# Rewriting a fused hybrid layer (short convolution plus latent attention) on eight cores: a new deal of the tokens, a new order of the stages, and row sums moved off TensorE

## The chip, the cores and the metric

The kernel runs on all 8 cores of one Trainium2 chip. Cores 0 to 3 (one die) work on the first sequence of the batch, cores 4 to 7 (the other die) on the second, and no core talks to another. The metric is device time in microseconds (us) of the slowest core.

Executions come in two states. In the fast one, all cores have nearly the same granted TensorE clock and nearly the same span (0.975 to 0.978 and 3345.0 to 3367.5 us in the profiled run of before). In the slow one, the cores of one die or of both have a lower clock and the time is longer (one die at 0.806 to 0.813 in the slowest run of before, 3942.61 us). A ratio is the mean time of one kernel's fast runs over that of the other's fast runs of the same rounds on the same chip, so it is not quite the ratio of the medians that are quoted.

## The reference, cut to what matters

```python
D_MODEL, BATCH, SEQ, CHUNK = 4096, 2, 4096, 64
N_HEADS, Q_LORA, KV_LORA, ROPE_DIM = 16, 1024, 512, 64     # nope and value: 128 per head

xn = rmsnorm(x, g_in)
proj = xn @ w_in
gB, gC, h, z_conv, c_q, c_kv, k_rope, z_attn = split(proj)
y_conv = gB * causal_short_conv(gC * h, conv_w) * silu(z_conv)     # depthwise, width 3
q = rmsnorm(c_q, q_norm_g) @ w_uq          # 16 heads of 128 + 64
kv = rmsnorm(c_kv, kv_norm_g) @ w_ukv      # 16 heads of 128 + 128
# rope on q_pe and on the one shared k_rope; mask by chunks: key_chunk <= query_chunk
attn = softmax(q k^T / sqrt(192), masked) @ v
y = concat(y_conv, attn * silu(z_attn))
out = rmsnorm(x + y @ w_out, g_final)
```

A core owns 1024 query tokens of its sequence, but needs the latent keys (`c_kv` and `k_rope`) of all 4096. The mask is causal by chunks of 64 tokens.

## The kernel before

Each core owns two blocks of 512 tokens: block k and block 7-k. It computes the stages in this order: latent keys of all 4096 tokens, query and gate projections, attention, convolution, output projection. Between them stand barriers, and the convolution reads x again, since attention takes its room.

Latent keys, with the features on the partitions (the weights are the stationary operand, 512 tokens stream through):

```python
for m in range(5):                       # 4 tiles of c_kv, 1 of duplicated rope columns: 640
    for kc in range(32):
        mm(psb[bank], WCKV[:, kc, m*128:(m+1)*128], XG[xb][:, kc, :], ...)
# sum of squares: 32 more matmuls per slot with a matrix of ones
mm(psb[0], ones_bf, xsq[stb][:, j, :], ...)
...
mm(psb[4], dmat, tk, True, True, ...)    # fp32 product that adds the rope halves
```

Attention, per head and key tile. One program serves all cores, so blocks that a core's mask forbids are computed too and set to zero by a bias in the exponential (`gate`). The row sums of the softmax are a third matmul, with a matrix of ones:

```python
units = [(0, 0), (1, 1), (2, 2), (3, None)]            # block bi == 0: (slot, gate column)
# bi == 1: [(0..3, None), (4, 3), (5, 4), (6, 5), (7, None)]; 48 key tiles of 128 per head
mm(psb[bank][:, c0:512], KH[...], QN[...]); mm(psb[bank][:, c0:512], K2[...], TQ[...])
P.add("act", ... activation(out=PT[pb], in_=psb[bank], func=AF.Exp, bias=gate[:, gc:gc+1]))
mm(psb[po][:, c0:512], VH[...], PT[pb][:, c0:512], ...)
mm(psb[pl][:, c0:512], ones_bf, PT[pb][:, c0:512], ...)      # row sums
```

Output projection, in two passes of 512 tokens, each of which reads all of `w_out` (4 MB per column tile of 512, 8 column tiles):

```python
for grp in range(2):
    for ct in range(8):
        for kg in range(8):
            ... mm(psb[pbase + tt], ysrc, wo[:, kcc, :], kc == 0, kc == 31)
    # norm of 4 row tiles, then the stores
```

The softmax here doesn't subtract the row's maximum and nothing guards it: scores larger than these inputs give would overflow.

Of the kernel before, what the change touches and what calls it, by code (L numbers as in the profile page):

```python
# [6 lines left out]
F32 = mybir.dt.float32  # L7
BF16 = mybir.dt.bfloat16
# [5 lines left out]
D = 4096  # L14
S = 4096
BLK = 512
NMT = 93
EPS = 1e-6
ATTN_SCALE = 192 ** -0.5
ORDER = [0, 1, 2, 4, 5, 6, 3, 7]  # L20
NEG = -30000.0

class Tr:
    __slots__ = ("lastw", "readers", "sem", "cnt", "name")

    def __init__(self, name=""):
        self.lastw = None
        self.readers = []
        self.sem = None
        self.cnt = 0  # L30
        self.name = name

class Ins:
    __slots__ = ("eng", "fn", "deps", "signal", "ordinal", "dma_tr", "dma_val")

    def __init__(self, eng, fn, deps):
        self.eng = eng
        self.fn = fn
        self.deps = deps
        self.signal = False  # L40
        self.ordinal = 0
        self.dma_tr = None
        self.dma_val = 0

ENGS = ("pe", "act", "dve", "pool", "sp")

class Prog:
    def __init__(self):
        self.ins = {e: [] for e in ENGS}
        self.last = {e: None for e in ENGS}  # L50
        self.dma_trs = []
        self.sync_same_engine = True

    def _deps(self, eng, reads, writes):
        deps = []
        for t in reads:
            if t.lastw is not None:
                deps.append(t.lastw)
        for t in writes:
            if t.lastw is not None:  # L60
                deps.append(t.lastw)
            deps.extend(t.readers)
        out = []
        for d in deps:
            if d[0] == "c":
                i = d[1]
                if i.eng == "pe" and eng == "pe":
                    continue
                if i.eng == eng and not self.sync_same_engine:
                    continue  # L70
                i.signal = True
            out.append(d)
        return out

    def add(self, eng, fn, reads=(), writes=()):
        ins = Ins(eng, fn, self._deps(eng, reads, writes))
        ev = ("c", ins)
        for t in reads:
            t.readers.append(ev)
        for t in writes:  # L80
            t.lastw = ev
            t.readers = []
        self.ins[eng].append(ins)
        self.last[eng] = ins
        return ins

    def dma(self, eng, fn, reads=(), writes=(), sem_tr=None):
        ins = Ins(eng, fn, self._deps(eng, reads, writes))
        if sem_tr is None:
            sem_tr = writes[0]  # L90
        if sem_tr not in self.dma_trs:
            self.dma_trs.append(sem_tr)
        sem_tr.cnt += 16
        ins.dma_tr = sem_tr
        ins.dma_val = sem_tr.cnt
        ev = ("d", sem_tr, sem_tr.cnt)
        for t in reads:
            t.readers.append(ev)
        for t in writes:
            t.lastw = ev  # L100
            t.readers = []
        self.ins[eng].append(ins)
        return ins

    def barrier(self):
        evs = []
        for e in ("pe", "act", "dve", "pool"):
            if self.last[e] is not None:
                self.last[e].signal = True
                evs.append(("c", self.last[e]))  # L110
        for t in self.dma_trs:
            evs.append(("d", t, t.cnt))
        for e in ENGS:
            self.ins[e].append(Ins(e, None, list(evs)))

    def emit(self, nc, stack):
        esem = {e: stack.enter_context(nc.semaphore("sem_" + e)) for e in ("pe", "act", "dve", "pool")}
        for i, t in enumerate(self.dma_trs):
            t.sem = stack.enter_context(nc.semaphore("dsem%d" % i))
        for e in ("pe", "act", "dve", "pool"):  # L120
            n = 0
            for i in self.ins[e]:
                if i.signal:
                    n += 1
                    i.ordinal = n
        block = stack.enter_context(nc.Block())

        def run(ename, eng):
            waited = {}
            for i in self.ins[ename]:  # L130
                for d in i.deps:
                    if d[0] == "c":
                        sem, val, key = esem[d[1].eng], d[1].ordinal, d[1].eng
                    else:
                        sem, val, key = d[1].sem, d[2], id(d[1])
                    if waited.get(key, 0) >= val:
                        continue
                    waited[key] = val
                    eng.wait_ge(sem, val)
                if i.fn is None:  # L140
                    continue
                r = i.fn(eng)
                if i.dma_tr is not None:
                    r.then_inc(i.dma_tr.sem, 16)
                elif i.signal:
                    r.then_inc(esem[ename], 1)
# [21 lines left out]
R_XG = 0  # L168
R_Y = 65536
R_CKVN = 131072  # L170
R_K2 = 163840
R_CQG = 172032
R_MISC = 188416
ARENA = 188416 + 20480 + 2048

def build_program(dbg=False):
    nc = bass.Bass("TRN2", target_bir_lowering=False)
    P = Prog()

# [3 lines left out]
    xT = din("xT", [8, 128, 32, 512])  # L183
    xres = din("xres", [1024, D])
    xh = din("xh", [128, 32, 4])
    cs_tab = din("cs_tab", [8, 128, 512])
    gate_d = din("gate", [128, 6])
    w_in_t = din("w_in_t", [NMT, 128, 32, 128])
    w_uq_t = din("w_uq_t", [16, 128, 8, 256])
    w_ukv_t = din("w_ukv_t", [8, 128, 4, 512])  # L190
    w_out_t = din("w_out_t", [8, 8, 128, 4, 512])
    g_in_d = din("g_in_t", [128, 32])
    g_q_d = din("g_q_t", [128, 8])
    g_kv_d = din("g_kv_t", [128, 4])
    convw_d = din("convw_t", [128, 48])
    gfin_d = din("gfin_b", [128, D])
    dmat_d = din("dmat", [128, 128])
    out = nc.dram_tensor("out", [1024, D], F32, kind="ExternalOutput").ap()

    stack = contextlib.ExitStack()  # L200
    with stack:
        arena = stack.enter_context(nc.sbuf_tensor("arena", [128, ARENA // 4], F32))
        psb_t = [stack.enter_context(nc.psum_tensor("psb%d" % i, [128, 512], F32)) for i in range(8)]
        psb = [t[:, :] for t in psb_t]
        tps = [Tr("ps%d" % i) for i in range(8)]

        def v32(off, n):
            return arena[:, off // 4: off // 4 + n]

        def v16(off, n):  # L210
            return arena[:, off // 4: off // 4 + n // 2].bitcast(BF16)

        mo = [R_MISC]

        def misc32(n):
            a = v32(mo[0], n)
            mo[0] += 4 * n
            return a

        def misc16(n):  # L220
            a = v16(mo[0], n)
            mo[0] += 2 * n
            return a

        g_in_t = misc32(32)
        g_q_t = misc32(8)
        g_kv_t = misc32(4)
        convw = misc32(48)
        gate = misc32(6)
        ssq = misc32(32)  # L230
        tot = misc32(4)
        rfin = misc32(4)
        rbh = misc32(4)
        rbh2 = misc32(4)
        uh = misc32(4)
        dmat = misc32(128)
        ones_bf = misc16(128)
        rb = [misc32(512) for _ in range(2)]
        cs = [misc32(512) for _ in range(2)]
        rqb = [misc32(512) for _ in range(2)]  # L240
        csq = [misc32(512) for _ in range(2)]
        rkvb = misc32(512)
        assert mo[0] <= ARENA, mo[0]
        t_const = Tr("const")
        t_rb = [Tr(), Tr()]
        t_cs = [Tr(), Tr()]
        t_rqb = [Tr(), Tr()]
        t_csq = [Tr(), Tr()]
        t_rkvb = Tr()
        t_small = Tr("small")  # L250

        XG = [v16(R_XG + b * 32768, 16384).rearrange("p (k t) -> p k t", k=32) for b in range(2)]
        t_xg = [[Tr() for _ in range(8)] for _ in range(2)]
        Y = v16(R_Y, 32768).rearrange("p (f t) -> p f t", f=32)
        t_y = [[Tr() for _ in range(2)] for _ in range(32)]
        CKVN = v16(R_CKVN, 16384).rearrange("p (k t) -> p k t", k=4)
        t_ckvn = [Tr() for _ in range(8)]
        K2 = v16(R_K2, 4096)
        t_k2 = [Tr() for _ in range(8)]
        CQG = v16(R_CQG, 8192).rearrange("p (k t) -> p k t", k=8)  # L260
        t_cqg = [[Tr() for _ in range(2)] for _ in range(8)]

        for dst, src in ((g_in_t, g_in_d), (g_q_t, g_q_d), (g_kv_t, g_kv_d), (convw, convw_d),
                         (gate, gate_d), (dmat, dmat_d)):
            P.dma("sp", lambda e, dst=dst, src=src: e.dma_start(out=dst, in_=src), writes=[Tr()])
# [101 lines left out]
        for _ in load_slot(0):  # L367
            pass
# [495 lines left out]
```

## Time and profile before

The time before was 3382.11 us (median of 3 runs, 3380.28 to 3384.14). These are the first lines of the profile's page of the kernel before, and its chain of waits: the span, the busy time of each engine with its share and number of instructions, and the engines' shares of the chain that ended last.

```profile
span 3367.5 us, 49842 instructions; the slowest of 8 cores (3345.0 to 3367.5 us)
PE 3026.4 (90%) x15163; PEld 1421.8 (42%) x15456; DVE 861.4 (26%) x1359; ACT 852.0 (25%) x1356; POOL 151.0 (4%) x249
PE 84%; DMA 11%; DVE 2%; issue 2%; ACT 1%; SPq 0%; DVEq 0%; ACTq 0%; POOLq 0%
```

TensorE (PE) is the bound: busy for 90% of the span and 84% of the chain (PEld are its own weight loads; they overlap its matmuls, since 3026.4 and 1421.8 us together are more than the span). No other engine is busy for a third of it. What the average hides is where TensorE stands still, and that a cut by stages shows. This is the view of time windows of core 6, cut at the stage boundaries: start and end, length, busy us of each engine, granted TensorE clock, share of DMA time, GB/s. The windows are, in this order: start, latent keys, query and gate projection, attention, the hole after it, convolution, output projection, tail.

```profile
0.00:102.90 102.90, 16.19 (x32) 2.22 (x33) 20.18 (x41) 23.00 (x22) 8.74 (x9) 1.00 0.97 172
102.90:470.00 367.10, 345.60 (x1521) 153.24 (x1552) 186.68 (x309) 140.24 (x138) 0.00 (x0) 0.99 0.47 156
...
486.90:855.60 368.70, 337.77 (x1521) 151.37 (x1552) 48.45 (x67) 32.12 (x50) 14.75 (x21) 1.00 0.37 66
...
865.00:1847.50 982.50, 968.82 (x5032) 490.17 (x5120) 300.46 (x444) 540.77 (x897) 10.57 (x20) 1.00 0.10 21
1847.50:1907.90 60.40, 1.02 (x33) 1.10 (x35) 22.34 (x41) 1.86 (x3) 2.11 (x3) 0.54 0.73 192
1907.90:2818.70 910.80, 904.28 (x5018) 423.78 (x5118) 183.11 (x317) 63.39 (x111) 42.84 (x61) 1.00 0.40 71
...
2837.20:3329.00 491.80, 452.55 (x2007) 199.78 (x2048) 66.79 (x97) 46.22 (x126) 65.55 (x124) 0.98 0.98 187
3329.00:3367.50 38.50, 0.08 (x1) 0.00 (x0) 24.98 (x36) 1.92 (x7) 0.00 (x0) 0.56 0.52 218
```

Attention and convolution are matmuls without a gap (968.82 of 982.50 us, 904.28 of 910.80): only fewer columns make them shorter. Start, hole and tail are stretches in which TensorE does next to nothing, 202 us together; the short gaps that are left out (16.9, 9.4 and 18.5 us) add 45. In the output stage TensorE is idle for 39 us while the DMA queues are busy 98% of the time, and the view of waits names the loads of `w_out` (24 waits, 55.2 us, of which the longest, 18.5 us, is the gap before the stage):

```profile
PE psb L269 <- DMA arena<-w_out_t: 55.2, 24, 18.5
```

A line of the waits reads: engine, tile and line, what it waited for, then us in total, number of waits, and the longest. The size of a matmul comes from the trace too: 49 back-to-back matmuls of 512 columns take 10.74 us, 219 ns each, about 0.43 ns per column.

### The profile page before, as it was taken

Reading aid. Unit: us, or ns where it says so; the run is one execution under the profiler, and the core shown is the slowest. Engines: PE = TensorE matmul, PEld = TensorE weight load, DVE = VectorE, ACT = ScalarE, POOL = GpSimd, SP = SyncE. Lnnn points to the kernel's source line nnn. Section 1 sums busy time; section 2 is a strip of 40 time slices with the busy share of each in tenths; the row PEclk is TensorE's granted clock in tenths of the full one; section 3 lists DMA queues with packets and bytes.
Section 4 is the critical chain, followed back from the end, with each engine's and each line's share of the span. In section 5 each row is a group of like instructions: output and inputs, shape, how many; then the busy total and the mean of one; then the engine's idle time right before and its main releaser. Section 6 shows DMA issues by size and latency. Waiting matters only on the chain.

```text
span 3367.5 us, 49842 instructions; the slowest of 8 cores (3345.0 to 3367.5 us)
## 1 busy us (share of the span) xinstructions
PE 3026.4 (90%) x15163; PEld 1421.8 (42%) x15456; DVE 861.4 (26%) x1359; ACT 852.0 (25%) x1356; POOL 151.0 (4%) x249
## 2 busy tenths in 40 slices
PE   1799977899899999999999399999999997998895
PEld 0344433344444554554554144444444443443342
DVE  2355531200223232332332221212121211003003
ACT  2244410100355546456456000000000000110110
POOL 0000000000000000000000000000000000111110
PEclk9999989999999999999999699999999998999997
DMA  9556523343111011011100544444444445999996
GB/s 186 137 179 200 187 38 63 63 76 63 38 29 23 13 29 23 14 29 23 23 7 10 151 76 76 76 76 75 73 73 74 73 75 109 190 184 203 201 174 176
DMA packets 103895, 302.26 MB, mean 90 GB/s; under 512 B 28496, under 2 KB 28752, under 8 KB 102480
## 3 DMA queue, kind: packets, MB, share of 16 engines
q0 software_dynamic: 66384, 177.23, 30.8%
q1 hardware_dynamic: 37248, 121.83, 11.6%
q8 instruction: 128, 2.10, 0.3%
q14 instruction: 135, 1.11, 0.1%
HBM read 459.46 MB, written 16.78 MB: 141 GB/s over the span
## 4 chain that ended last, share of the span: by engine, by line
PE 84%; DMA 11%; DVE 2%; issue 2%; ACT 1%; SPq 0%; DVEq 0%; ACTq 0%; POOLq 0%
PE psb L269 84%; DMA arena<-w_out_t 5%; DMA arena<-w_in_t 3%; DMA arena<-xT 2%; DVE arena L754 1%; DVE arena L412 0%; ACT arena L416 0%; ACT arena L320 0%; DMA arena<-w_uq_t 0%; DVE arena L347 0%; DVE arena L349 0%; DVE arena L360 0%; DVE arena L317 0%; DVE arena L356 0%; DVE arena L570 0%
## 5 line engine op out<-in xcount | busy, mean ns | idle before, releaser
L269 PE MATMUL psb<-arena 128*128 128x512 bf16 (+3 forms) x15163 | 3026.4, 357 | 302.7 <-DMA arena<-w_in_t 72.0
L269 PEld LDWEIGHTS psb<-arena 128*128 128x128 bf16 x15456 | 1421.8, 98 | 1906.8 <-issue 394.7
L560 ACT ACTIVATE arena<-psb,arena 128x512 bf16<-128x512 f32 x384 | 259.5, 687 | 158.4 <-PE psb L269 158.4
L556 ACT ACTIVATE arena<-psb 128x512 bf16<-128x512 f32 (+3 forms) x384 | 204.4, 544 | 99.0 <-PE psb L269 99.0
L320 ACT ACTIVATE arena<-arena 128x1024 bf16<-128x1024 f32 x128 | 133.9, 1056 | 207.0 <-PE psb L269 123.8
L564 DVE MEMSET arena<- 64x64 bf16 x128 | 14.3, 112 | 571.9 <-ACT arena L556 571.5
L743 ACT ACTIVATE arena<-arena 128x512 bf16<-128x512 f32 x64 | 40.3, 630 | 460.5 <-DVE arena L740 454.8
L740 DVE TENSOR_TENSOR arena<-psb,arena 128x512 f32<-128x512 f32 x64 | 43.5, 690 | 433.6 <-PE psb L269 392.7
L399 POOL DMA_DIRECT2D arena<-w_in_t x88 | 61.8, 703 | 1758.7 <-PE psb L269 1201.1
L659 DVE TENSOR_TENSOR arena<-psb,arena 128x512 f32<-128x512 f32 x32 | 22.0, 687 | 405.6 <-PE psb L269 355.3
L504 ACT ACTIVATE arena<-psb 128x512 bf16<-128x512 f32 x128 | 76.4, 597 | 177.6 <-PE psb L269 177.6
L317 DVE TENSOR_SCALAR arena<-arena 128x512 bf16<-128x512 f32 x256 | 106.2, 476 | 44.0 <-DMA arena<-xT 44.0
L412 DVE TENSOR_TENSOR arena<-psb,arena 128x512 f32<-128x512 f32 x48 | 33.2, 691 | 329.0 <-PE psb L269 329.0
L570 DVE RECIPROCAL arena<-psb 128x512 f32<-128x512 f32 x32 | 107.4, 3357 | 17.2 <-PE psb L269 17.2
L518 DVE CAST arena<-psb 128x512 bf16<-128x512 f32 x128 | 88.2, 691 | 79.3 <-PE psb L269 73.0
L690 ACT ACTIVATE arena<-arena 128x512 f32<-128x512 f32 x32 | 20.1, 629 | 341.8 <-DVE arena L688 341.8
L715 POOL DMA_DIRECT2D arena<-w_out_t x128 | 67.7, 529 | 470.9 <-PE psb L269 403.6
L424 ACT ACTIVATE arena<-arena 128x512 bf16<-128x512 f32 x32 | 20.1, 629 | 192.1 <-DVE arena L412 192.0
L688 DVE TENSOR_TENSOR arena<-psb,arena 128x512 f32<-128x512 f32 x32 | 22.0, 687 | 174.9 <-PE psb L269 174.9
L343 DVE TENSOR_TENSOR arena<-psb,arena 128x512 f32<-128x512 f32 x32 | 22.1, 690 | 169.4 <-PE psb L269 169.3
L656 ACT ACTIVATE arena<-psb 128x512 f32<-128x512 f32 x32 | 17.4, 594 | 183.4 <-PE psb L269 183.4
L664 ACT ACTIVATE arena<-psb 128x4 f32<-128x4 f32 x16 | 2.8, 173 | 219.6 <-PE psb L269 219.6
(54 smaller groups left out, 529.0 us busy)
## 6 DMA issues: line engine op xcount, KB each, us to landing
arena<-w_in_t POOLq DMA_DIRECT2D x93, 1024.0 KB, 7.9
arena<-xT SPq DMA_DIRECT2D x144, 512.0 KB, 5.0
arena<-w_out_t POOLq DMA_DIRECT2D x128, 512.0 KB, 8.3
arena<-xres SPq DMA_DIRECT2D x16, 1024.0 KB, 18.7
out<-arena SPq DMA_DIRECT2D x8, 2048.0 KB, 11.1
arena<-xT SPq DMA_DIRECT2D x32, 256.0 KB, 2.7
arena<-w_uq_t POOLq DMA_DIRECT2D x16, 512.0 KB, 5.8
arena<-w_ukv_t POOLq DMA_DIRECT2D x8, 512.0 KB, 5.1
```

The lines of the kernel that those rows point to most:

```text
L269: P.add("pe", lambda e: e.matmul(out_, lhsT, rhs, start=start, stop=stop), reads=reads, writes=writes)
L317: P.add("dve", lambda e, xb=xb, kc=kc, stb=stb, j=j: e.tensor_scalar(out=XG[xb][:, kc, :], in0=xst[stb][:, j, :], scalar1=g_in_t[:, kc:kc ...
L320: P.add("act", lambda e, stb=stb: e.activation(out=xsq[stb], in_=xst[stb], func=AF.Square), reads=[t_xst[stb]], writes=[t_xsq[stb]])
L399: P.dma("pool", lambda e: e.dma_start(out=dst, in_=w_in_t[m], max_dma_last_dim=8192), writes=[tdst])
L504: P.add("act", lambda e, bank=bank, hb=hb, s=s: e.activation(out=KH[hb][:, s * 512:(s + 1) * 512], in_=psb[bank], func=AF.Copy), reads=[tp ...
L518: P.add("dve", lambda e, bank=bank, s_=s_, half=half: e.tensor_copy(out=VH[:, 4 * s_ + 2 * half:4 * s_ + 2 * half + 2, :], in_=psb[bank].r ...
L556: P.add("act", lambda e, bank=bank, pb=pb, c0=c0: e.activation(out=PT[pb][:, c0:512], in_=psb[bank][:, c0:512], func=AF.Exp, scale=ATTN_SC ...
L560: P.add("act", lambda e, bank=bank, pb=pb, gc=gc: e.activation(out=PT[pb], in_=psb[bank], func=AF.Exp, scale=ATTN_SCALE, bias=gate[:, gc:g ...
L570: P.add("dve", lambda e, pl=pl, bi=bi: e.reciprocal(out=rc[bi], in_=psb[pl]), reads=[tps[pl]], writes=[t_rc[bi]])
L715: P.dma("pool", lambda e: e.dma_start(out=WO[i % 4], in_=w_out_t[ct, kg], max_dma_last_dim=8192), writes=[t_wo[i % 4]])
L740: P.add("dve", lambda e, pbase=pbase, tt=tt, ct=ct, xb=xb: e.tensor_tensor(out=Ht[tt][:, ct * 512:(ct + 1) * 512], in0=psb[pbase + tt], in ...
L743: P.add("act", lambda e, tt=tt, ct=ct: e.activation(out=JUNK, in_=Ht[tt][:, ct * 512:(ct + 1) * 512], func=AF.Square, accum_out=ssq[:, tt ...
```

## The change

Its intent: compute less on TensorE and leave no hole between the stages.

- Chunks of 64 tokens are dealt round-robin to the four cores of a sequence. Then every core's queries see nearly the same share of the keys, and attention becomes a triangle of 64-column steps for all of them, masked by one small minimum per diagonal step.
- Latent keys are computed with the tokens on the partitions (x stationary, 576 columns of weights stream). The norm is then a scalar per partition, and TensorE transposes put the result back. Of 32 tiles of 128 tokens, 8 are the core's own: they come as fp32 and are also scaled and kept for the later stages; 24 are others', cast to bf16 by the DMA.
- The convolution comes before attention, so x is read once; its result is parked in DRAM.
- The row sums of the softmax become fp32 additions on VectorE; two matmuls per block finish them. Projections of the next head fill the steps of the present one.
- The output projection reads `w_out` once, for all 8 row tiles; the first 5 column tiles of the residual sum are parked in DRAM and read back at the end.

The diff has 1808 lines; this is its core, with cuts marked.

```diff
-ORDER = [0, 1, 2, 4, 5, 6, 3, 7]                     # blocks of 512 tokens
+    own = [(0, t) for t in range(8)]
+    oth = [(a, m) for a in (1, 2, 3) for m in range(8)]
+    seq = oth[:4]                                    # then own and others in turn
+    for t in range(8):
+        seq += [own[t], rest[t]]
 ...
-                    mm(psb[bank], WCKV[:, kc, m * 128:(m + 1) * 128], XG[xb][:, kc, :], ...)
+            mm(psum[:, A, 0:256], x_, WC[:, kc, 0:256], kc == 0, kc == 31)
+            mm(psum[:, B, 0:320], x_, WC[:, kc, 256:576], kc == 0, kc == 31)
 ...
+        def prep(T, c):                              # a quarter of tile T
+            if a == 0:                               # an own tile
+                s = xst[nst[0] % 3]                  # ring of 3 fp32 buffers
+                load("sp", s[:, :, :], x_tile[T, :, c * 1024:(c + 1) * 1024]...)
+                tt(XG[:, 8 * c:8 * c + 8, ...], s[:, :, :], g_in..., ALU.mult)
+                act(xt, src, AF.Copy)
+            act(q[:, :]..., src, AF.Square)
+            tt(q[:, 0:512], q[:, 0:512], q[:, 512:1024], ALU.add)
+            tt(o[:, :], q[:, 0:256], q[:, 256:512], ALU.add)
+        def post(T):                                 # the norm step of tile T
+            act(junk..., lat, AF.Square, accum=st[:, 0:1])
+            ...
+            stt(t2[:, :], psum[:, B, 256:320], st[:, 4:5], cs[:, 64:128], ALU.mult, ALU.mult)
+            ...
+            load_cs(T + 3)                           # rope table, on the same queue as the xst loads
 ...
-                    mm(psb[pl][:, c0:512], ones_bf, PT[pb][:, c0:512], i == 0, i == n - 1, ...)
+            if i >= 8 * b_:
+                tt(pt[:, :, 0:64], pt[:, :, 0:64], gmask[:, :, :], ALU.min)
+            A = ACC[b_][:, :, off:512]
+            tt(A, A, pt[:, :, 0:w], ALU.add)         # fp32 row sums on VectorE
 ...
-        for grp in range(2):
-            for ct in range(8):
+        for ct in range(7):
+            for kg in range(8):
+                for t_ in range(8):
+                    out_mm(ct, kg, t_, (8 * ct + kg) % NW)
+            if ct < 5:
+                dma("sp", hsp[t_, :, ct * 512:(ct + 1) * 512], H, ...)       # park
+        for t_ in range(8):                          # last column tile, row by row
+            for kg in range(8):
+                out_mm(7, kg, t_, (56 + kg) % NW)
+            evac(7, t_)
+            finish_tile(t_)                          # norm, stores; reload(t_ + 3)
```

## The prediction

> **What bounds the kernel now.** TensorE. The chain of waits is 84% matmuls, and time windows split core 6's 3367.5 us span so: start 103 (TensorE idle 55 us for five weight loads in small packets), latent keys 367, query/gate projection 369 plus 17 before it, attention 982 plus 9, a hole of 60 (x read again, barrier), convolution 911 plus 18, output projection 492 (24 waits for w_out, 55 us), tail 38. 49 matmuls of 512 columns take 10.74 us, 219 ns each; stages without waits run at 0.42 to 0.435 ns per column, so I cost by counting columns.
>
> **Columns, before to after.**
> - Latent keys: 803k[...] to 590k (576 instead of 640 columns, sums of squares folded on VectorE). 367 to about 240 us.
> - Query/gate: 795k both; 28 us of waits for the ACT square go, since the ones-matmul is deferred. 369 to 337.
> - Attention: 2261k to 1655k. The ones-matmuls (369k) become VectorE additions, and the round-robin deal turns 48 key tiles per head, partly masked to zero, into a triangle: 17.4k instead of 23.0k columns for each product. At 0.4345 ns: 982 to 720, plus 30 for the first head's projections.
> - Convolution: 2097k plus 1024 tiny halo matmuls to 2130k. 911 to 905.
> - Output: 1049k both, but w_out is read once instead of twice. 492 to 444.
>
> **Gaps.** The barriers and the re-read of x go (17+9+60+18 = 104 us, 5 left). The start loads contiguous rows: an estimate from 312 GB/s (plain queue, bytes over its share) and 170 GB/s (casting queue) is 55 to 65 us, instead of 103. The tail finishes tile by tile: 15 instead of 38.
>
> **New costs.** VectorE in attention becomes nearly as long as TensorE. From traced 692 ns per 512 fp32 elements I estimate per head: row-sum additions 22, masks 5, evictions 8, finishing 6 = 41 us against TensorE's 45.[...] In narrow steps with V evictions VectorE is longer and TensorE waits for the mask: 2 us a head, 40 with the last head, which has nothing to fill in. ScalarE needs about 31 us a head: no bound. Ln and Exp alternate there[...] I charge no table loads. In the latent stage ScalarE (1056 ns per 1024 elements) needs 15.5 us per pair of tiles against TensorE's 17: close. The spill of h adds 21 MB of traffic, hidden.
>
> **Sum.** 65 + 240 + 905 + 337 + 30 + 720 + 40 + 5 + 444 + 15 = 2801, with 15 us between span and time and 24 unforeseen: 2840 us. Range 2775 to 2950. Faster by over 2%: 0.97; within 2%: 0.02; slower: 0.01.
>
> **Right if:** TensorE busy above 94% of the span; attention 760 to 800 us with VectorE above 85% busy; convolution about 905; output stage about 445 with DMA below 90% busy; no table load per Ln.
>
> **Wrong if:** VectorE queues evictions and masks behind 1.2 us additions, so attention is VectorE-bound (+50 to +100); the latent stage is bound by DMA (2 MB each 8.5 us) or ScalarE (+30 to +60); matmuls of 256 and 320 columns don't hide their 98 ns weight loads (+20)[...]. Lower than the range only if column cost falls below 0.42 ns.

The 41 us of VectorE rest on the traced 692 ns. ScalarE's 31 us a head is an estimate that the text does not derive; in the run ScalarE was busy 395.42 us in attention, 24.7 a head.

## The result, and the profile after

The kernel after took 2975.01 us (median of 4 runs, 2931.45 to 3036.95) and was correct. Two of the four runs were fast, 2937.51 and 2931.45 us. The other two had one die at a mean clock of 0.926 to 0.938 and spans of 2990 to 3035 us on that die, while the other die kept 0.97 and some 2920 us. The ratio of fast runs to the fast runs of before is 0.8676, 95% interval 0.866 to 0.8693. The same lines of the page, after:

```profile
span 2936.0 us, 40663 instructions; the slowest of 8 cores (2913.7 to 2936.0 us)
PE 2706.9 (92%) x15672; PEld 1494.5 (51%) x15672; DVE 1129.3 (38%) x2105; ACT 719.2 (24%) x1113; POOL 183.8 (6%) x348
PE 76%; DVE 8%; DMA 8%; issue 4%; ACT 3%; DVEq 0%; SPq 0%; ACTq 0%; POOLq 0%
```

TensorE still bounds it, but its share of the chain fell from 84% to 76%: work was taken from TensorE, and something else became longer. The windows of core 2 (same columns) show where. They are: the start, latent keys in two parts, convolution, query and gate projection, the first head's projections, attention and its last head.

```profile
0.00:88.00 88.00, 41.24 (x263) 27.51 (x264) 28.19 (x70) 20.60 (x21) 17.98 (x37) 0.77 0.86 187
88.00:355.00 267.00, 175.50 (x1395) 132.78 (x1394) 138.46 (x396) 123.91 (x189) 12.69 (x24) 0.83 0.47 108
355.00:454.80 99.80, 94.44 (x877) 76.22 (x875) 59.43 (x221) 55.70 (x91) 11.10 (x21) 1.00 0.75 128
454.80:1358.40 903.60, 903.58 (x5126) 502.23 (x5127) 180.27 (x259) 39.18 (x48) 67.11 (x127) 1.00 0.47 79
1358.40:1693.40 335.00, 335.00 (x1554) 151.86 (x1552) 44.87 (x57) 33.30 (x51) 24.84 (x47) 1.00 0.48 78
1693.40:1725.00 31.60, 31.21 (x210) 20.26 (x208) 14.86 (x23) 8.25 (x12) 0.53 (x1) 1.00 0.11 18
1725.00:2395.00 670.00, 645.84 (x4003) 365.28 (x4003) 535.73 (x899) 360.35 (x527) 12.69 (x24) 1.00 0.11 20
2395.00:2444.80 49.80, 36.75 (x207) 17.90 (x206) 40.92 (x71) 26.81 (x39) 2.65 (x5) 0.96 0.59 157
```

Put beside the terms of the prediction (stage boundaries are the first and last matmul of a stage in the trace; the hole before a stage is counted with it):

| stage | before | predicted | after |
|---|---|---|---|
| start and latent keys | 470.0 | 305 (65 + 240) | 454.8 |
| convolution | 971.2 | 905 | 903.5 |
| query and gate | 385.6 | 337 | 335.0 |
| attention | 991.9 | 790 (30 + 720 + 40) | 751.3 |
| output, to the last matmul | 510.3 | 444 | 443.2 |
| tail | 38.5 | 15 | 48.2 |
| gaps | (in the stages) | 5 | (none) |
| span | 3367.5 | 2801 | 2936.0 |

The gain of 431.5 us is 240.6 in attention, 67.7 in the convolution, 67.1 in the output, 50.6 in query and gate, 15.2 in latent keys, less 9.7 in the tail. Three terms met their number within 2 us. One was 39 us too high. Two were too low, by 150 and 33 us. In the window from 88 to 355 us no engine and no queue is near its limit (TensorE 175.50, VectorE 138.46, ScalarE 123.91 of 267 us, DMA share 0.47), yet it is the stretch that overran: an overrun that no busy time explains. The output stage and the tail are shown with experiment 8.

### What the chain shows in the latent stage

This is the chain of waits of the kernel after between 85 and 130 us: the shares by line of the program, then pieces as start, us, and what they were. L448 is the cast of an own tile's quarter, L453 its square, L482 to L490 the norm step, xst the ring of three fp32 buffers, cst the rope table.

```profile
by line: DMA xst_75<-x_tile 34.5%; DMA cst_103<-cs_key 18.3%; issue 9.3%; DMA xst_74<-x_tile 8.9%; ACT sq_85 L453 4.6%; ACT sq_84 L453 3.5%; DVE CKVN L514 2.9%; DVE XG L445 2.7%; ACT xb_72 L448 2.3%; DVE sq_85 L454 1.9%; DVE t_101 L489 1.9%
...
113.72 0.20 DVE t_102 L490
113.99 0.33 SPq L364
114.37 6.95 DMA xst_75<-x_tile
121.40 1.06 ACT xb_72 L448
122.46 0.95 ACT sq_84 L453
123.48 8.56 DMA xst_75<-x_tile
```

The reader sees a ring, not a limit. The norm step's last use of a rope table (L490) lets the SP queue issue the table's next load. Behind it in the same queue stand the loads of the next own tile, which land 7 to 9 us after their issue. Only then can ScalarE cast and square the quarter, and the next norm step stands behind that in ScalarE's order. The queue's own waits and TensorE's waits between 88 and 355 us fit this:

```profile
SPq L215 <- DVE t_102 L490: 192.8, 20, 13.4
```

```profile
PE ps L326 <- DVE ckn_93 L492: 61.9, 7, 11.3
```

The queue stood for 192.8 of 267 us in front of a table load, with x loads queued behind. A long wait of the queue is no proof by itself: in experiment 1, where no x load stands behind the table loads any more, the queue waits even longer (103 to 379 us of that run) and the stage is 76 us shorter:

```profile
SPq L215 <- DVE t L485: 239.3, 28, 11.0
```

What counts is what stands behind the wait. TensorE's transposes (L326) waited 61.9 us for the norm step. Own tiles took 19.7 to 22.5 us each after the first, the tiles between them 8.7 to 11.8, the later tiles mostly 8.3. The plan was 17 us for a pair; after the first pair it got 30 to 34. The mean granted clock was 0.83 in that window and 1.00 in the next, where the waits are few. So part of the overrun may be clock; how much was not separated.

### The profile page after: what moved, and what is told of

It reads as the page before. It is cut to its first block, busy times and chain, and to the rows that moved or that the text cites. A ratio compares the mean times of both kernels' runs of the same rounds, so it can differ in the third digit from the quotient of the medians.

```text
span 2936.0 us, 40663 instructions; the slowest of 8 cores (2913.7 to 2936.0 us)
## 1 busy us (share of the span) xinstructions
PE 2706.9 (92%) x15672; PEld 1494.5 (51%) x15672; DVE 1129.3 (38%) x2105; ACT 719.2 (24%) x1113; POOL 183.8 (6%) x348
## 4 chain that ended last, share of the span: by engine, by line
PE 76%; DVE 8%; DMA 8%; issue 4%; ACT 3%; DVEq 0%; SPq 0%; ACTq 0%; POOLq 0%
PE ps L644 31%; PE ps L934 13%; PE ps L710 8%; PE ps L694 4%; PE ps L769 3%; PE ps L760 3%; PE ps L464 3%; PE ps L898 3%; PE ps L825 3%; PE ps L824 3%; DVE ACC_148 L895 3%; PE ps L463 2%; DMA wst_78<-w_ckv 2%; DMA xst_75<-x_tile 1%; DMA xst_76<-x_tile 1%
## 5 line engine op out<-in xcount | busy, mean ns | idle before, releaser
L644 PE MATMUL ps<-XG,ws_110 128*128 128x384 bf16 (+2 forms) x1760 | 316.0, 341 | 3.9 <-DVE ckn_93 L492 3.9
L644 PE MATMUL ps<-XG,ws_111 128*128 128x384 bf16 (+2 forms) x1696 | 299.1, 338 | 0.0
L644 PE MATMUL ps<-XG,ws_112 128*128 128x512 bf16 (+2 forms) x1664 | 298.6, 341 | 0.0
L644 PEld LDWEIGHTS ps<-XG,ws_110 128*128 128x128 bf16 x1760 | 173.0, 98 | 143.2 <-issue 7.1
L644 PEld LDWEIGHTS ps<-XG,ws_111 128*128 128x128 bf16 x1696 | 165.8, 98 | 129.5
L644 PEld LDWEIGHTS ps<-XG,ws_112 128*128 128x128 bf16 x1664 | 162.8, 98 | 132.1
L824 PE MATMUL ps<-QN_136,KH_132 128*128 128x512 bf16 (+7 forms) x384 | 115.8, 318 | 0.0
L825 PE MATMUL ps<-TQ_138,K_64 128*128 128x512 bf16 (+7 forms) x384 | 115.8, 318 | 0.0
L825 PE MATMUL ps<-TQ_137,K_64 128*128 128x512 bf16 (+7 forms) x384 | 115.2, 317 | 0.0
L824 PE MATMUL ps<-QN_135,KH_131 128*128 128x512 bf16 (+7 forms) x384 | 115.2, 317 | 0.0
L883 ACT ACTIVATE PT_139<-ps 128x1024 bf16<-128x1024 f32 x96 | 84.6, 881 | 99.1 <-PE ps L825 99.1
L463 PE MATMUL ps<-WC,xb_70 128*128 128x256 bf16 x256 | 75.1, 309 | 30.3 <-DMA xb_70<-x_tile 11.4
L883 ACT ACTIVATE PT_141<-ps 128x768 bf16<-128x768 f32 (+1 forms) x96 | 70.9, 739 | 107.9 <-PE ps L825 107.7
L883 ACT ACTIVATE PT_140<-ps 128x896 bf16<-128x896 f32 (+1 forms) x96 | 77.8, 810 | 72.6 <-PE ps L825 72.2
L463 PE MATMUL ps<-WC,xb_72 128*128 128x256 bf16 x256 | 73.6, 304 | 17.3 <-ACT xb_72 L448 11.4
L710 PE MATMUL ps<-XG,ws_110 128*128 128x512 bf16 x384 | 84.0, 379 | 0.0
L464 PE MATMUL ps<-WC,xb_70 128*128 128x320 bf16 x256 | 79.4, 342 | 0.0
L464 PE MATMUL ps<-WC,xb_72 128*128 128x320 bf16 x256 | 77.5, 336 | 0.0
L710 PE MATMUL ps<-XG,ws_112 128*128 128x512 bf16 x320 | 69.9, 379 | 0.0
```

The source lines that it names most:

```text
L463: mm(psum[:, A, 0:256], x_, WC[:, kc, 0:256], kc == 0, kc == 31)
L464: mm(psum[:, B, 0:320], x_, WC[:, kc, 256:576], kc == 0, kc == 31)
L644: mm(o, w[:, kc, :], XG[:, kc, c0:c1], kc == 0, kc == 31)
L710: mm(o, w[:, kc, :], XG[:, kc, c0:c0 + 512], kc == 0, kc == 31)
L824: mm(o, KH[h % 2][:, k0:k0 + 128], QN[h % 2][:, c0:c0 + w], True, False)
L825: mm(o, K2[:, k0:k0 + 128], TQ[h % 2][:, c0:c0 + w], False, True)
```

## The experiments

All twelve change the kernel after. Before was run beside each on the same chip. Stage times are from the trace of each run's profiled execution, all of them fast. Their noise can be read from the seven kernels whose latent stage is the same (after, e3, e3b, e4, e5, e9, e11): start and latent keys took 448.8 to 455.2 us, and the fifth tile started at 94.2 to 98.9 us. Differences of some 6 us in that stage are therefore not read.

### 1. Own tiles cast in flight (e1_cast_own)

```diff
         def prep(T, c):
             if a == 0:
-                s = xst[nst[0] % 3]
-                load("sp", s[:, :, :], x_tile[T, ...])
-                tt(XG[...], s[:, :, :], g_in..., ALU.mult)
-                act(xt, src, AF.Copy)
+                tt(XG[...], xt, g_in..., ALU.mult)      # xt: loaded and cast by the DMA like any other tile
 ...
-            if T < 32 and TILES[T][0] != 0:
+            if T < 32:
                 load_other(T)
```

> The changed kernel, but the core's own 8 tiles of x come through the casting queue, whole and four tiles ahead like the other 24, and XG is made from the bf16 copy. The fp32 staging ring of three, its loads on the plain queue behind the rope-table loads, and the ScalarE copy are gone. Theory LATENCY (the 267 us from 88 to 355 hold 130 us more than predicted, because each own tile exposes two landings of 7 to 9 us one after the other, and the latent-norm step of the tile before waits behind it in ScalarE's order): the stretch falls to about 140 us, so the first convolution matmul comes at about 325 us instead of 455, and the time goes from 2933 to about 2805 us. Rival BANDWIDTH (the DMA engines limit the stage): the same bytes are read from memory, so no more than 20 us. Rival SCALAR (ScalarE limits it): it does 34 us less copying, so at most 34 us.

Measured: ratio 0.8467 (0.8452 to 0.8482), median 2861.22 us, correct. Start and latent keys fell from 454.8 to 378.8 us; all other stages stayed within 2 us. After the second, own tiles took 11.6 to 13.3 us, the tiles between them 8.5. The largest of TensorE's waits that were left after 103 us:

```profile
PE ps L326 <- DVE ckn L487: 19.1, 8, 3.0
```

So the ring through the fp32 buffers, with ScalarE's cast behind it, cost 76 us, more than the 34 us that the rival SCALAR allowed. The same bytes of x are read from DRAM in less time, so bandwidth was not the bound. The gain is less than was expected: about 3 us per own tile and the late start remain.

### 2. The fp32 ring kept, its loads issued earlier (e2_early_xst)

```diff
+                if nst[0] == 0:
+                    for j in range(3):
+                        load_own(j)
-                load("sp", s[:, :, :], x_tile[T, :, c * 1024:(c + 1) * 1024]...)
 ...                                                  # at the end of prep:
+            if a == 0:
+                load_own(nst[0] + 2)                 # refill as soon as a buffer is read
```

> The changed kernel with one thing moved: the load into a staging buffer of an own tile is issued as soon as that buffer is free, up to three pieces ahead, instead of behind the rope-table load of the tile before. Bytes, buffers and ScalarE's work stay. Theory LATENCY: of the two landings that each own tile exposes, the first goes and the second (fourth piece, three buffers) partly stays: 9 to 13 us for each of 8 pairs, so 70 to 105 us less, about 2830 to 2865 us. Rival SCALAR: nothing, as ScalarE has the same work. Rival BANDWIDTH: nothing.

Measured: ratio 0.8573 (0.8557 to 0.8588), correct; the mean of its three fast runs is 2897.5 us. Start and latent keys: 417.5 us, 37 less than the kernel after. After the first, own tiles took 15.2 to 18.9 us, the tiles between them 8.5. TensorE's waits for a cast quarter (20.3 us in the kernel after) are gone, and its wait for the norm step fell from 61.9 to 51.7 us:

```profile
PE ps L326 <- DVE ckn L503: 51.7, 10, 7.2
```

ScalarE's work is unchanged here (each quarter is still cast and squared), so the 37 us come from the order of the loads alone. The gain is about half of what the first experiment gave, and below the range expected: the rest went only when the cast and the ring went. How it splits between the three-buffer ring and ScalarE's cast was not separated.

### 3. The tail: half the rows get their last two column tiles late (e3_tail, e3b_tail)

The idea was to finish the first four row tiles while TensorE still has a stage of work, at the cost of reading 4 MB of `w_out` a second time.

```diff
-        wl = [(ct, kg) for ct in range(8) for kg in range(8)]
+        wl = [(ct, kg) for ct in list(range(8)) + [6] for kg in range(8)]
 ...
-        for ct in range(7):
+        for ct in range(6):
 ...     # then: column tile 6 of rows 0-3; tile 7 of rows 0-3 with finish_tile;
 ...     # tile 7 of rows 4-7; tile 6 of rows 4-7 with finish_tile
+            if t_ == 0:
+                reload(3)                            # e3b only: before its use
```

> The changed kernel with the last two column tiles of the output projection reordered: tile 6 then 7 for the first half of the tokens, tile 7 then 6 for the second half, so that the first four token tiles are finished 55 us before the end. w_out of tile 6 is read twice (4 MB more). Theory DMA-BOUND TAIL (the last stretch moves 23.4 MB at 325 GB/s in 72 us, of which only 25 us can lie under the matmuls): the time from the last matmul to the end falls from 46 us to about 12, and the kernel is 25 to 40 us faster, about 2900 us. Rival CHAIN (the tail is the serial chain of sum, square root, reciprocal and scaling of the last tile): the last tile's chain is unchanged, so under 5 us gained.

The first version gave a wrong result (relative error 0.38), so its time counts for nothing: row tile 3 was finished before its parked values were read back, a mistake of the experiment. Its trace already showed a tail of 24.3 us and an output stage of 455.6.

> e3_tail mended: there one spilled tile was reloaded after its use (wrong result), and late weight loads stood behind reloads that waited for an output buffer. Theory DMA-BOUND TAIL: the engines were 99% busy from 2780 us to the end in e3 and still are, since the order adds 4 MB of weights to the 23.4 MB of the tail; so a small gain only: 10 to 25 us faster than 2933, and the result is right. Rival CHAIN: none of it.

The mended version was correct: ratio 0.8658 (0.8644 to 0.8672). Beside the early reload of tile 3 it also moves the reloads of tiles 4 to 6. The tail went from 48.2 to 22.2 us, the output stage from 443.2 to 458.4: 26 won, 15 given back, within the 10 to 25 us expected. The extra 4 MB keep the queues full (DMA share 0.97 from 2780 to 2840 us and 0.95 from there to 2895), and TensorE waits for weights instead (12.1 us in 4 waits). Finishing rows earlier is right; paying for it in traffic is not.

### 4. Row sums back on TensorE (e4_ones_back)

```diff
-            A = ACC[b_][:, :, off:512]
-            tt(A, A, pt[:, :, 0:w], ALU.add)
+            for p in range(2):
+                mm(bank(7)[:, off:512], ones16[:, :], pt[:, p, 0:w], i == 0 and p == 0, last and p == 1)
 ...     # key evictions move from ScalarE to VectorE, one bank less for projections
```

> The changed kernel with one part of the change undone: softmax row sums are again made by matmuls with ones on TensorE (278 thousand columns more, 33 thousand of the folding matmuls less), not by additions on VectorE; K evictions go to VectorE, which is thereby freed. Theory TENSOR (attention is bound by TensorE, with 37 us of waits for VectorE inside it): attention grows by 245 thousand columns at 0.4345 ns = 107 us, less up to 37 us of waits: 70 to 107 us slower, 3003 to 3040 us. Rival VECTOR (VectorE is the limit of attention, so the additions cost as much as they save): within 30 us of 2933.

Measured: ratio 0.9023 (0.9007 to 0.904), correct. Attention took 869.4 us instead of 751.3: this part of the change is worth 118 us, above the 70 to 107 us expected. The attention windows of this run and of the kernel after (columns as above) show the exchange:

```profile
1692.40:2561.80 869.40, 829.26 (x5121) 463.89 (x5120) 300.92 (x639) 333.83 (x448) 14.86 (x28) 1.00 0.13 29
```

```profile
1693.40:2444.80 751.40, 713.80 (x4418) 403.44 (x4416) 591.50 (x991) 395.42 (x576) 15.86 (x30) 1.00 0.14 29
```

VectorE falls from 591.50 to 300.92 us busy and TensorE rises by 115.5. The rival, that VectorE is the bound of this stage, falls: halving VectorE's work made the stage longer. That the growth is above the range has two parts: the added columns cost 115.5 us and not 107, and TensorE's idle time did not shrink (40.1 us after 37.6). The edit also takes one of the two PSUM banks of the projections, and 19.7 us of its waits are at the projections (L769, L778); so not all of the 118 us need be the row sums themselves.

### 5. Value evictions on ScalarE (e5_v_act)

```diff
-            evq.append(lambda: cp(VH[p % 2][...], o...))
+            evq.append(lambda: act(VH[p % 2][...], o..., AF.Copy))
```

> The changed kernel with one engine swapped: the V evictions of attention go to ScalarE (0.60 us each) instead of VectorE (0.69 us). Theory MASK QUEUE (TensorE's waits in attention, 23 us for masked tiles and 11 us for V evictions, come from VectorE's order: an eviction and a 1.2 us addition ahead of the mask): most of those 34 us go, the kernel is 15 to 35 us faster than 2933, about 2900 to 2918. Rival LATENCY OF THE MASK ITSELF (exp, then mask, then product, whatever else VectorE does): no change, and since ScalarE now does more ahead of each exp, perhaps some us slower.

Measured: ratio 0.8636 (0.8623 to 0.8648), correct. Attention took 734.0 us, 17 less. The waits tell which of VectorE's jobs TensorE had waited for. After (attention, start to end):

```profile
PE ps L898 <- DVE PT_141 L890: 16.6, 20, 2.6
PE ps L760 <- DVE VH_134 L779: 5.7, 7, 0.9
PE ps L760 <- DVE VH_133 L779: 4.8, 6, 0.8
PE ps L898 <- DVE PT_139 L890: 4.4, 5, 2.0
```

With the evictions on ScalarE (whole run):

```profile
PE ps L898 <- DVE PT L890: 24.1, 34, 2.6
```

The waits for an eviction (L779) are gone. The waits for the mask (L890) are not: 16.6 + 4.4 + 1.4 + 0.9 = 23.3 us over the four buffers before the edit, 24.1 after. In the run with the row sums on TensorE the value product (L885 there) still waited 17.3 us for the mask, though the additions were gone from VectorE. So taking work away from VectorE does not take these waits away. That they are the length of one narrow step itself (exponential, mask and product follow each other, and too little other work stands ready) fits this and is argued, not shown: in this experiment ScalarE does more ahead of each exponential, which could hide a gain at the mask. Experiment 8 (e11) shows that wider steps more than halve TensorE's idle time.

### 6. The late start and the scalings (e6_latent, e8_latent2)

Both keep the cast in flight of experiment 1 and do two more things. The 32 scalings of the weights, which VectorE did in one block, are put between the groups of matmuls that use them, so that VectorE frees ScalarE's two square buffers sooner. And the four scalings of an own tile move: in e6 to the tile's own turn, ahead of its first half of matmuls, in e8 behind the next tile's squares and the transposes.

```diff
-        for i in range(16):                           # 32 scalings, then the first matmuls
+        def wc_part(i):
 ...
         for c in range(4):
+            for i in range(4 * c, 4 * c + 4):
+                wc_part(i)
 ...
             post(T - 1)
+            scale_own(T)                              # e6
 ...
                 pe_trans(T - 1)
+            scale_own(T)                              # e8, instead
```

> As e1_cast_own, with two more changes of order. First, the 32 scalings of the latent weights no longer stand on VectorE ahead of every folding of squares: they are interleaved with the four pieces of the first four tiles. Second, an own tile's scaling into XG stands on VectorE behind the latent-norm step of the tile before. Theory ORDER (in e1 ScalarE's squares stood still from 21 to 62 us since their two buffers wait for VectorE, which works through weights in order of their landing; and each own tile still took 11.6 instead of 8.5 us since 7.7 us of scaling stood ahead of the norm step): the fifth tile starts at 75 to 85 us instead of 102, own tiles take under 9.5 us, the first convolution matmul comes at 325 to 345 us instead of 379, total 2810 to 2830 us against e1's 2861. Rival BYTES (the start is bound by its 18 MB): the fifth tile still starts at 95 us or later.

Measured (e6): ratio 0.8464 (0.845 to 0.8477), median 2855.02 us, correct. The fifth tile starts at 92.5 us instead of 97.4 (102.6 in e1). The stage is 372.5 us, 6 less than e1, at the edge of the noise. Both are short of what was expected (75 to 85 us, and a stage of 325 to 345): the first own tile grew from 16.6 to 20.0 us and took part of the earlier start back. The other own tiles are now the fast ones (8.8 us), but the tile after each takes 11.0 to 12.7.

> As e6_latent, but the scaling of an own tile into XG stands on VectorE after the folding of the next tile's squares and the copies of the transposed latents, not ahead of them. In e6 the tile after each own one took 11 to 12.7 us instead of 8.5: ScalarE's squares waited for their two buffers behind 4.9 us of scaling, and the norm step of the own tile stood on ScalarE behind those squares. Theory ORDER: tiles after the start take under 10 us each, 16 to 25 us less than e6 in the latent stage, so 2828 to 2838 us against e6's 2855. Rival VECTOR WORK (the scaling costs its time wherever it stands): within 6 us of e6.

Measured (e8): ratio 0.8455 (0.8441 to 0.8468), correct. The stage is 368.9 us: within 4 us of e6, with the same pattern (8.8, then 10.9 to 12.6). Between 100 and 250 us of e6 VectorE is busy 110.28 of 150 us. Moving the work in the order only moves which tile is slow, so the order theory missed. That the amount of VectorE's work is what is left was the rival; it is consistent with this, and experiment 9 tried it. Another rival was not tried: between 120 and 260 us of e6 ScalarE waits 47.4 us for one of its two square buffers, which VectorE has to free, and a third buffer could show whether it is these waits.

### 7. The three together (e7_all)

The edits of e6, of e5, and the mended tail of e3b.

> All mends together: e6_latent, e3b_tail and e5_v_act. They lie in separate stages, so if each theory holds the gains add: latent 105 to 120 us, tail 10 to 25, attention 15 to 35, that is about 2760 to 2800 us. If the gains do not add, a stage waits for something shared.

Measured: ratio 0.8388 (0.8376 to 0.84), median 2828.98 us, correct; latent 369.4, attention 736.6, output 457.9, tail 26.7. By the ratios the single gains (e6, e5 and e3b together 0.027) add up to within a few us of what e7 shows (0.029), but most had been expected larger, so the time is above the range expected.

### 8. The tail without extra traffic (e9_tail2ct) and the triangle undone (e11_full)

In e9 the last two column tiles run row by row. Both tiles' weights stay in the SBUF (six more weight buffers), so a row tile takes twice as long to compute and is finished at half the rate.

```diff
+             48 * KB, 52 * KB, 56 * KB, 60 * KB, Z_R + 12 * KB, Z_R + 46 * KB])]    # 16 weight buffers
 ...
-        for ct in range(7):
+        for ct in range(6):
 ...
         for t_ in range(8):
-            for kg in range(8):
-                out_mm(7, kg, t_, (56 + kg) % NW)
-            evac(7, t_)
+            for ct in (6, 7):
+                for kg in range(8):
+                    out_mm(ct, kg, t_, (8 * ct + kg) % NW)
+                evac(ct, t_)
             finish_tile(t_)
```

> The changed kernel with another end: the last two column tiles (not one) of the output projection are done token tile by token tile, so that finished rows appear every 14 us, not every 7, over the last 110 us. w_out is still read once; 16 weight slots fit since the last two column tiles of h need rings of three, not eight buffers. Theory DMA-BOUND TAIL (23.4 MB at 325 GB/s need 72 us after the first finished row): these now lie under 96 us of matmuls. The output stage stays at 443 us, the stretch after the last matmul falls from 48 to 12 to 20 us, the kernel is 28 to 36 us faster than 2933. Rival CHAIN: under 5 us. If weights come late as in e3 and e3b, the output stage grows.

Measured: ratio 0.8616 (0.8602 to 0.8631), correct. The output stage stays at 443.2 us and the tail is 20.5, 28 us less than after. The mean of the fast runs is 2907.8 us, 27 less than the 2934.5 of after, just under the 28 to 36 expected. To see why, first the end of the kernel after: pieces of its chain of waits, then the windows from the first finished row tile to the last matmul, and from there to the end.

```profile
2854.21 11.03 DMA out<-RR_190
2865.80 16.74 DMA RR_190<-hsp
2885.59 18.20 DMA out<-RR_190
2904.32 12.52 DMA RR_190<-hsp
```

```profile
2847.00:2887.70 40.70, 40.70 (x190) 18.43 (x189) 25.13 (x32) 4.07 (x12) 2.12 (x3) 1.00 0.98 257
2887.70:2936.00 48.30, 0.42 (x2) 0.00 (x0) 17.19 (x21) 3.05 (x9) 1.40 (x2) 0.53 0.76 268
```

Buffer RR_190 goes round: store, reload, scale, store, reload. From 2847 us on, 16.78 MB of results must be written and 6.55 MB of parked sums (5 of the 8 row tiles) read back, 23.3 MB; between 2848 and 2920 us the trace shows a DMA share of 0.98 at a mean of 291 GB/s. At that rate the 23.3 MB take 80 us, an estimate, and TensorE covers only 40.7 of them (DMA share 0.98). (The 325 GB/s of the expectations were too high for the whole stretch; the trace comes near them only after the last matmul, with 329 GB/s from 2887.7 to 2920 us.) In e9 the same traffic is spread over the last two column tiles:

```profile
2733.00:2886.00 153.00, 153.00 (x711) 69.30 (x709) 51.65 (x65) 19.96 (x54) 9.33 (x15) 1.00 0.71 206
2886.00:2906.40 20.40, 0.34 (x2) 0.00 (x0) 5.89 (x7) 1.02 (x3) 0.00 (x0) 0.58 0.26 103
```

TensorE has no gap, the DMA share is 0.71, and after the last matmul only one row tile is left. The tail was a matter of how much traffic had to fit under how many matmuls. That the three RR buffers, each waiting for its store before its reload, were a bound of their own was not tested with a fourth buffer; the DMA share of 0.98 speaks against it.

In e11 all products of attention run at the full 512 columns, with the probabilities outside the triangle set to zero by GpSimd.

```diff
-                mm(o, KH[...], QN[h % 2][:, c0:c0 + w], True, False)
+                mm(o, KH[...], QN[h % 2][:, 512 * b_:512 * b_ + 512], True, False)
 ...
-                mm(bank(4 + b_)[:, off:512], VH[...], pt[:, p, 0:w], ...)
+                mm(bank(4 + b_), VH[...], pt[:, p, :], ...)
```

> The changed kernel with another part undone: scores and value products run over all 512 queries of a block in every step, as in the kernel before for its masked key tiles, and the columns that the triangle leaves out are set to zero by GpSimd. 344 thousand columns more on TensorE; exp, masks and sums as in the changed kernel. Theory TENSOR (attention costs its columns): 344 thousand at 0.4345 ns = 149 us, less up to 37 us of waits that the longer steps hide: 112 to 149 us slower, 3045 to 3082 us. Rival VECTOR (narrow steps are bound by VectorE, so columns there are free): under 80 us slower.

Measured: ratio 0.9021 (0.9003 to 0.9038), correct; attention 867.6 us, 116 more than with the triangle; the mean of the fast runs is 3044.8 us, at the lower edge of the 3045 to 3082 expected. Its attention window:

```profile
1691.60:2559.30 867.70, 850.48 (x4418) 428.77 (x4416) 602.20 (x991) 397.41 (x576) 133.08 (x254) 1.00 0.12 25
```

TensorE's busy time grows by 136.7 us for 344k more columns (0.40 ns each), and its idle time falls from 37.6 to 17.2: the wide steps hide part of the waits. So the stage is TensorE's, and part of what the triangle saves in columns comes back as waits at its narrow steps.

### 9. Everything that helped, and the scalings on GpSimd (e12_pool)

The edits of e8, e5 and e9, and one more: the four scalings of an own tile go to GpSimd.

```diff
                     tt(XG[:, 8 * c:8 * c + 8, ...], xb[T % 4][:, 8 * c:8 * c + 8, :],
-                       g_in..., ALU.mult)
+                       g_in..., ALU.mult, eng="pool")
```

> Everything that helped, in one kernel: own tiles cast in flight, the start with the weight scalings between the squares, V evictions on ScalarE, and the last two column tiles of the output run row by row as in the earlier tail-only run. From the single runs the attention stage should take 734 to 737 us and the tail about 20 us after the last matmul with the output stage at 443 us. One thing is new, and tells two theories of the latent stage's remaining 28 us or so apart: the scaling of an own tile (four steps of about 1.22 us on VectorE) goes to GpSimd. VECTOR WORK (the tile after an own tile is slow because VectorE has some 16 us of work in each 17 us pair): the pairs fall to within 1 us of 17 us, the latent stage from 369 to 340 to 355 us, the whole to about 2775 to 2795 us, a ratio of 0.822 to 0.829. Rival CHAIN (the tile after is slow because of the order of its norm step, whatever VectorE has to do; or GpSimd[...] holds back the loads that it issues): latent stays at 365 to 385 us, the whole at 2795 to 2815 us.

Measured: ratio 0.838 (0.8368 to 0.8393), median 2831.53 us, correct. Attention 734.4, output 442.9 and tail 21.2 us are as expected. The latent stage is not: 394.5 us, longer than with either theory, 25.6 more than e8. The tile after an own tile now takes 8.5 us, but the own tile 15.0 to 16.0. The timeline of VectorE and of GpSimd around one own tile (start, us, engine, line, operation, form) shows why:

```profile
145.77 0.28 DVE L489 SCALAR_TENSOR_TENSOR t<-ps,stat,cst 128x64 f32<-128x64 f32 x1
145.96 0.15 DVE L354 RECIPROCAL stat<-stat 128x1 f32<-128x1 f32 x1
146.22 0.75 DVE L491 SCALAR_TENSOR_TENSOR ckn<-ps,stat,gkv 128x512 bf16<-128x512 f32 x1
146.88 5.18 DVE L495 TENSOR_TENSOR kr<-t,t 128x64 bf16<-128x64 f32 x2
```

```profile
144.38 7.45 POOL L453 TENSOR_TENSOR XG<-xb,g_in 128x1024 bf16<-128x1024 bf16 x4
```

The first of the two narrow additions (L495), 0.22 us long elsewhere, took 5.04 us and ended when GpSimd's four scalings ended, at 151.9 us. This happened in 7 of the 8 own tiles, 5.04 us each time, and in the eighth another addition with both inputs in SBUF (L446) took 3.7 us instead of 0.42. Operations with one input in PSUM (L489, L491) and the reciprocals ran beside GpSimd at their usual length. So in this trace the additions that were held had both inputs in SBUF, as GpSimd's scalings have, and the wait lasted through the whole series of back-to-back GpSimd operations, not to the end of the one that was under way: they follow each other every 1.86 us, and the addition of 146.88 us came in the second. Why is not shown. (The same scaling took 1.22 us on VectorE in e7_all.)

The test of the work theory is therefore inconclusive. The follower's slowness did go with VectorE's scalings (11 to 12.6 us down to 8.5), which fits it, but the new wait hides what the pair would take. No run was left to try another engine or to run this kernel with the scalings on VectorE. From the parts that ran (e8's latent 368.9 us and e12's other stages, 2436.5 us) such a kernel should have a span near 2805 us; this is an estimate, not a run. Of what ran, e7_all and e12_pool are the fastest, and both beat before and after.

## Why the prediction was right or wrong, point by point

The time fell in the range: 2840 predicted, 2775 to 2950, against 2931 and 2938 us in fast runs. But that is partly luck: its reserve (15 + 24 us), one term that was counted twice (30 us) and a range open to 2950 covered a miss of 150 us in one stage.

- **"Latent keys: 803k ... to 590k ... 367 to about 240 us"** and the start of 65 us: wrong, 454.8 in place of 305 us. This is the step that failed. Columns were counted right, but columns don't bound this stage. The stage was checked against each engine's and the queues' capacity (ScalarE 15.5 us of a pair's 17), and not for how the steps wait for each other: an order with SP loads behind a table load behind a norm step, with three buffers. Casting in flight took 76 us out (e1), earlier loads alone 37 (e2). The listed risk, "bound by DMA ... or ScalarE (+30 to +60)", was the right stage and the wrong cause: DMA share was 0.47, ScalarE 46% busy. Some 32 us of the miss is the start (97.4 instead of 65 us for the fifth tile). With the weight scalings moved (e6, e7, e8, e12) that tile started 5 to 13 us earlier, but outside e12 the first own tile grew from 14.2 to some 20 us and took much of it back. The risk that matmuls of 256 and 320 columns don't hide their weight loads did not come: later tiles take 8.3 us for 18.4 thousand columns, 0.45 ns each.
- **"Convolution: ... 911 to 905", "Query/gate: ... 369 to 337", "Output: ... 492 to 444"**: right, 903.5, 335.0 and 443.2 us. Where the trace shows TensorE without gaps, columns times the traced 0.43 ns predict to within 1%.
- **"At 0.4345 ns: 982 to 720, plus 30 for the first head's projections"**: mis-sized. The 1655k columns already held the projections of all 16 heads, so the 30 us were counted twice. 1655k columns at 0.4345 ns are 719 us; TensorE was busy 713.8. "TensorE waits for the mask: ... 40" was nearly right: 37.6 us idle, of which e5 shows that the waits for evictions (10.5 us) were the smaller part.
- **"VectorE in attention becomes nearly as long as TensorE"**, above 85% busy: too high. It was busy 535.73 of 670 us, 80%, and 591.50 us over the whole stage, 37 us a head and not 41. Added up by line of the program, a head has 20.9 us of row-sum additions (22 predicted), 3.5 of masks (5), 8.2 of evictions (8) and 6.3 of finishing (6): 38.9 us, and the records of neighbours overlap by the rest. So it is mainly the masks (0.22 us each) that were overestimated. The addition itself took 0.69 us per 512 elements, as in the kernel before, and 1.22 us per 1024.
- **"I charge no table loads"**: right. The trace has six table loads of 1.28 us in the whole run and none per Ln: attention has 32 Ln, each with an Exp after it (L842, L843), and one table load.
- **"The tail finishes tile by tile: 15 instead of 38"** and **"21 MB of traffic, hidden"**: wrong, 48.2 us. Most of the parking is hidden, but the 6.55 MB read back and all 16.78 MB of stores met in the last 89 us. e9 removed 28 us by giving the same traffic more matmuls to hide under.
- **"with 15 us between span and time and 24 unforeseen"**: the profiled run's time was 1.5 us above its span; the reserve was used up by the latent stage.
- **"TensorE busy above 94% of the span"**: 92%; the missing part is the latent stage. Output with "DMA below 90% busy": right for most of the stage, wrong in its last 41 us (0.98).

What stays open: the residue of about 3 us per pair in the latent stage, the mask waits of 24 us, how e2's remainder splits, and why some executions fall in the slow state. In the four runs each that the first comparison holds, before had no slow run and after two, too few to say that the change makes it likelier. In the profiled fast run of the kernel after all eight cores have a granted clock of 1.00 in the convolution (500 to 1350 us).

## What to carry to other kernels

Counting columns is enough where TensorE runs without gaps (here to within 1%); where a stage passes data round through several engines and a queue, follow one tile round the ring with the traced latencies (here 7 to 9 us per load) before believing the sum of busy times. Don't put a load that must be early behind a load that waits for late work in the same queue (37 us here, by e2), and check in the queue's own waits that nothing stands behind it. At the end, divide the bytes still to move by the traced rate (291 GB/s here) and compare with the matmuls left to cover them. And before moving work to GpSimd, look at which VectorE operations beside it have both inputs in SBUF: here such an addition of 0.22 us took 5.04 us.
